# Opening a two-level matrix product with P1 and P2, and forming its operands one stage earlier

## The chip, the core and the metric

The program runs on one core of a Trainium2 chip. The metric is the device time of one execution in microseconds; the kernel before was timed at 2541.81 us (median of three runs, 2538.8 to 2543.2). The core has TensorE (PE in the rows, PEld for its weight loads), VectorE (DVE), ScalarE (ACT), GpSimd (POOL) and SyncE (SP, which here only issues transfers). Matmuls accumulate in PSUM, eight banks of 128 x 512 float32.

## The reference, cut to what matters

One layer of a streaming encoder on 512 rows and 2048 channels, in float32. Two branches share a normalised input h, and their gated sum is multiplied by w_out:

```
proj = h @ w_in                                  # also gives the gate logits
y_a = o_a @ w_br_a                               # branch A, gated DeltaNet
u = silu(layernorm(u)) * silu(z_b)
y_b = u @ w_br_b                                 # branch B
gate_a, gate_b = split(sigmoid(gate_logits + b_gate))
mixed = (gate_a * y_a + gate_b * y_b) @ w_out
x = x + rmsnorm(mixed, g_post)
x = x + rmsnorm(sigmoid(x @ w_ple_gate) * e, g_ple)
```

## The kernel before, in words

**Arithmetic.** Every float32 product is done as three fast matmuls: each operand is split into a high part (a cast on ACT) and a low part (a subtraction on DVE), and hi x hi, hi x lo and lo x hi are summed in PSUM. Weights arrive by SP's transfers into `raw` tiles (pool `rawp`, three buffers of 128 x 1024) and are split into `w` tiles (pool `ring`, four buffers).

**Stages and order.** Channel-major products run as jobs (`gemm_cm`, L160 on): 48 matmuls of 512 columns into one PSUM tile `g`, then an evacuation function. Pool `gps` has two such banks, so one job's evacuation lies beside the next job. Generators that were spawned are advanced by `tick`, once per matmul, and take a step every so many ticks. A scheduler orders each engine's instructions beforehand, by readiness and then by program order; an instruction whose output buffer isn't free is put behind others.

**Branch B** (L890 to L904) has 16 gate tiles (`gate_b_tile`, evacuated by a sigmoid on ACT, L700) and 16 tiles of y_b (`evac_yb`: L824 multiplies the PSUM tile by its gate, L826 adds it to `mixed`). Gate tiles run two ahead of the y_b tiles, so the normalised input `hT`, which fills all 32 buffers of `hpool`, is needed until almost the end. Gates lie in pool `slots` (21 buffers, 16 of them hold `mixed`). Pools `lop` (23 buffers, `LOP`) and `s2` (17 buffers) hold, in this stage, the 32 split tiles of u (`uh`, `ul`).

**The w_out product** is done by two levels of halving, for two column pairs `jp` one after the other: seven products P1, Q5, P6, P7, P3, P2, Q4 in place of eight. Left operands are sums of quarters of `mixed` (A11, S1 to S4, A12, A22), formed by `split_a`, `split_b` and `split_c` (L845 to L888), the first of them at the end of branch B, the others beside the first products. Right operands are blocks b11, b12, b22, b21 of w_out or running sums of them (`t`, pool `s3`): t1 = b11 + b12 by a DVE addition of two loaded tiles (L972), the later ones by an accumulating transfer that POOL issues (`acc`, L964). Each 128 x 1024 right operand is split into a piece (L1016 on ACT, L1017 on DVE) that feeds 12 matmuls (L1040 to L1042). `rw` is one more load buffer, in `s3`. Pool `s3` lies where `lop` and `s2` were, and is free only when the last y_b tile's matmuls have ended.

## Time and profile before

| | |
|---|---|
| median of three runs | 2541.81 us |
| the profiled execution, its own time | 2539.74 us |
| its span, first to last instruction | 2537.1 us |
| TensorE busy | 2495.0 us (98%) |
| VectorE busy | 1652.4 us (65%) |
| ScalarE busy | 1056.8 us (42%) |
| TensorE's mean granted clock | 0.997 |

The time is read off one profiled execution. A busy share is a mean over the whole span, and stages differ: windows of the span show which engine is short of what where. A matmul's record is longer than the distance to the next one, since matmuls overlap; the distance of their starts is what counts, and idle time in a row is therefore a little less than the time lost.

### The profile page before, as it was taken

To read this page: it belongs to the slowest core of one execution; us is meant where nothing else is said; L and a number is where in the kernel's file an instruction comes from. 1 tells how busy PE (TensorE), PEld (TensorE's weight loads), DVE (VectorE), ACT (ScalarE), POOL (GpSimd) and SP (SyncE) were. 2 spreads that over 40 slices of the span, in tenths; PEclk is the share of its full clock that TensorE was granted. 3 is DMA by queue.
4 is the path that set the end of the run, shared out by engine and by line. 5 is a ranking of instruction groups with operands and counts; after the bars stand their busy time and mean duration, and the time that the engine had idled before them with its cause. 6 is when DMAs were issued, how large, how long until landed. Compare 5 with 4: busy or idle time off the path is not lost.

```text
span 2537.1 us, 32634 instructions
## 1 busy us (share of the span) xinstructions
PE 2495.0 (98%) x12202; PEld 2035.7 (80%) x12202; DVE 1652.4 (65%) x3092; ACT 1056.8 (42%) x2083; POOL 140.6 (6%) x151
## 2 busy tenths in 40 slices
PE   8999999999999999999999999999999999999998
PEld 7878787777878777888888888887888888787887
DVE  6765767666676765977786868947433334777644
ACT  6655455455555455322222222225422222544532
POOL 0100000000000000000000000002000000000000
PEclk9999999999999999999999999999999999999999
DMA  6322222222222222333333332442322332677552
GB/s 257 122 87 71 84 72 83 79 75 88 71 84 71 84 67 75 104 105 102 105 97 107 104 107 98 135 135 92 100 99 93 100 99 92 184 214 224 191 174 75
DMA packets 85406, 279.45 MB, mean 110 GB/s; under 512 B 9472, under 2 KB 9728, under 8 KB 85248
## 3 DMA queue, kind: packets, MB, share of 16 engines
q1 hardware_dynamic: 81792, 266.89, 31.5%
q0 software_dynamic: 2304, 8.39, 1.8%
q10 hardware_dynamic: 1152, 2.10, 0.3%
q8 instruction: 95, 1.56, 0.3%
q14 instruction: 63, 0.52, 0.1%
HBM read 262.66 MB, written 14.68 MB: 109 GB/s over the span
## 4 chain that ended last, share of the span: by engine, by line
PE 85%; DVE 9%; ACT 2%; issue 2%; DMA 1%; POOL 0%; SPq 0%; DVEq 0%; POOLq 0%; ACTq 0%
PE g L182 23%; PE g L180 23%; PE g L178 23%; DVE prod L591 2%; PE f L1197 2%; PE f L1198 2%; PE f L1196 2%; DVE w L126 2%; PE psS L469 1%; PE f L1041 1%; PE f L1042 1%; PE f L1040 1%; DVE VT L592 1%; DVE cv L406 1%; PE psB L464 1%
## 5 line engine op out<-in xcount | busy, mean ns | idle before, releaser
L182 PE MATMUL g<-hh,w 128*128 128x512 f32 x2320 | 919.4, 396 | 13.1 <-DVE w L126 13.1
L180 PE MATMUL g<-hl,w 128*128 128x512 f32 x2320 | 915.2, 394 | 0.0
L178 PE MATMUL g<-hh,w 128*128 128x512 f32 x2320 | 914.6, 394 | 0.0
L126 DVE TENSOR_TENSOR w<-raw,w 128x512 fp32r<-128x512 f32 x780 | 549.2, 707 | 483.9 <-ACT w L125 482.8
L125 ACT CAST w<-raw 128x512 fp32r<-128x512 f32 x780 | 478.4, 619 | 893.3 <-PE g L182 789.3
L182 PEld LDWEIGHTS g<-hh,w 128*128 128x128 f32 x2320 | 436.6, 188 | 106.6 <-DVE w L126 21.2
L180 PEld LDWEIGHTS g<-hl,w 128*128 128x128 f32 x2320 | 436.6, 188 | 87.3 <-issue 1.6
L178 PEld LDWEIGHTS g<-hh,w 128*128 128x128 f32 x2320 | 436.8, 188 | 82.9 <-issue 0.2
L673 DVE SCALAR_TENSOR_TENSOR uc<-sg,vec,uc 128x483 f32<-128x483 f32 (+15 forms) x480 | 351.3, 734 | 14.2 <-ACT uc L670 4.3
L406 DVE SCALAR_TENSOR_TENSOR cv<-g,vec,cv 128x511 f32<-128x511 f32 x144 | 107.0, 743 | 32.9 <-ACT cv L404 32.3
L178 PE MATMUL g<-oh,w 128*128 128x512 f32 x256 | 99.6, 389 | 0.0
L180 PE MATMUL g<-ol,w 128*128 128x512 f32 x256 | 99.6, 389 | 0.0
L182 PE MATMUL g<-oh,w 128*128 128x512 f32 x256 | 99.6, 389 | 0.0
L178 PE MATMUL g<-uh,w 128*128 128x512 f32 x256 | 99.6, 389 | 0.0
L180 PE MATMUL g<-ul,w 128*128 128x512 f32 x256 | 99.6, 389 | 0.0
L182 PE MATMUL g<-uh,w 128*128 128x512 f32 x256 | 99.6, 389 | 0.0
L591 DVE TENSOR_TENSOR prod<-UT,VT 128x2 f32<-128x2 f32 (+30 forms) x248 | 87.6, 353 | 7.2
L1041 PE MATMUL f<-wsp,oph 128*128 128x512 f32 x192 | 76.7, 400 | 4.2 <-DVE wsp L1017 4.2
L1197 PE MATMUL f<-w,xh 128*128 128x512 f32 x192 | 75.6, 394 | 2.0 <-DVE w L126 2.0
L1040 PE MATMUL f<-wsp,oph 128*128 128x512 f32 x192 | 75.0, 398 | 1.8 <-ACT wsp L1016 1.8
L1196 PE MATMUL f<-w,xh 128*128 128x512 f32 x192 | 75.8, 396 | 0.0
L1042 PE MATMUL f<-wsp,opl 128*128 128x512 f32 x192 | 75.8, 395 | 0.0
(298 smaller groups left out, 2682.4 us busy)
## 6 DMA issues: line engine op xcount, KB each, us to landing
raw<-in_w_in SPq DMA_DIRECT2D x290, 512.0 KB, 3.3
raw<-in_w_ple_gate SPq DMA_DIRECT2D x40, 512.0 KB, 4.1
raw<-in_w_out SPq DMA_DIRECT2D x35, 512.0 KB, 4.8
raw<-in_w_br_a SPq DMA_DIRECT2D x32, 512.0 KB, 3.3
raw<-in_w_br_b SPq DMA_DIRECT2D x32, 512.0 KB, 3.2
t<-in_w_out POOLq DMA_DIRECT2D x16, 512.0 KB, 7.0
rw<-in_w_out SPq DMA_DIRECT2D x9, 512.0 KB, 4.7
x<-in_x SPq DMA_DIRECT2D x8, 512.0 KB, 9.1
```

The costliest lines, as they stand in the source:

```text
L125: nc.scalar.copy(hi, rq)
L126: nc.vector.tensor_tensor(lo, rq, hi.bitcast(F32), ALU.subtract)
L178: mm(ps, wh, rh, start=(k == 0), stop=False)
L180: mm(ps, wh, rl, start=False, stop=False)
L182: mm(ps, wl, rh, start=False, stop=(k == NK - 1))
L406: nc.vector.scalar_tensor_tensor(y[:, s:], ps[:, 0:T - s], vv(w0 + 3 - s), y[:, s:], ALU.mult, ALU.add)
L591: nc.vector.tensor_tensor(pv_, um, vm, ALU.mult)
L673: nc.vector.scalar_tensor_tensor(y[:, s:], u[:, 0:T - s], vv(w0 + TAPS - 1 - s), y[:, s:], ALU.mult, ALU.add)
L1041: mm(ps, lh, wl[:, c], start=False, stop=False)
L1042: mm(ps, ll, wh[:, c], start=False, stop=kk == 7)
L1196: mm(ps[tt], lh, wh, start=k == 0, stop=False)
L1197: mm(ps[tt], lh, wl, start=False, stop=False)
```

## The change

What it does, part by part. Branch B: gate tiles run eight ahead (`AHEAD`), and each further gate tile comes after a y_b tile and not before it; the first two gates lie in `slots`, the other 14 in `s2`. After the ninth y_b tile a generator `split_mixed`, one step every 12 matmuls, forms nearly all left operands of three of four row groups (`combine`); the fourth group and the splits of S3 follow beside the first products of w_out, two steps per piece. For the first column pair, w_out's products run as P1 with P2 (plain loads of b11 and b21), then Q5 alone, then P6, P7, P3, then Q4 alone; t1 is formed by a plain transfer of b12 into `t` and an accumulating transfer of b11, with no DVE addition. Entries hand over their transfers when they are started, up to two entries ahead, and their additions when they are used. The second column pair keeps its products and DVE additions; its reload of x (`load_x_again`) goes to `slots` and not `hpool`, and stands after P6 and P3. In layer norm, `rstd` moves from `s2` to `lop` and one more `ul` tile (ten, not nine) to `s2`.

```diff
@@ -694,9 +694,9 @@
-    def evac_gate(dst, i, col):
+    def evac_gate(dst, i, col, pool=None):
         def f(ps):
-            gt = slots.tile([P, T], F32, tag="s", name="gt")
+            gt = (pool or slots).tile([P, T], F32, tag="s2" if pool else "s", name="gt")
             nc.scalar.activation(gt, ps, AF.Sigmoid, bias=vv(V_BG + col))
@@ -788,7 +788,7 @@
-        rstd = s2.tile([P, T], F32, tag="s2", name="rstd")
+        rstd = low(0, "rstd", F32)
...
-            ul = low(LOP if i < 32 - LOP else 0, "ul")
+            ul = low(LOP if i < 33 - LOP else 0, "ul")
@@ -842,63 +842,69 @@
-    def split_a():
...
+    def halves(k2):
+        for n in range(2):
+            yield 2 * k2 + n, slice(n * 256, n * 256 + 256)
+
+    def combine(k2):
+        ah = hpool.tile([P, T], F32R, tag="h", name="ah")
+        al = hpool.tile([P, T], F32R, tag="h", name="al")
+        for kk, c in halves(k2):
+            while not (kk in added and kk + 8 in added):
+                yield
+            nc.scalar.copy(ah[:, c], mixed[kk][:, LO])
+            nc.vector.tensor_tensor(al[:, c], mixed[kk][:, LO], ah[:, c].bitcast(F32), ALU.subtract)
+            yield
+        AW["A11"][k2] = (ah, al)
+        for kk, c in halves(k2):
+            CC[kk] = sw_split(hpool, "h", mixed[kk + 8])
+            yield
+        s1 = slots.tile([P, T], F32, tag="s", name="sf")
+        for kk, c in halves(k2):
+            nc.vector.tensor_tensor(s1[:, c], mixed[kk][:, HI], mixed[kk + 8][:, HI], ALU.subtract)
+        AW["S1"][k2] = sw_split(hpool, "h", s1)
+        yield
+        s3_ = slots.tile([P, T], F32, tag="s", name="sf")
+        s4 = slots.tile([P, T], F32, tag="s", name="sf")
+        for kk, c in halves(k2):
+            nc.vector.tensor_tensor(s3_[:, c], mixed[kk][:, LO], mixed[kk][:, HI], ALU.subtract)
+            nc.vector.tensor_tensor(s1[:, c], s1[:, c], mixed[kk][:, LO], ALU.subtract)
+        yield
+        for kk, c in halves(k2):
+            nc.vector.tensor_tensor(s4[:, c], mixed[kk + 8][:, LO], s1[:, c], ALU.add)
+        AW["S2"][k2] = sw_split(slots, "s", s1)
+        yield
+        AW["S4"][k2] = sw_split(slots, "s", s4)
+        Sf[k2] = s3_
+        yield
+
+    def split_mixed():
+        for k2 in range(3):
+            yield from combine(k2)
+
+    def split_s3():
         for k2 in range(4):
...
+            AW["S3"][k2] = sw_split(s3, "s3", Sf.pop(k2))
             yield
 
     order = [k + 8 * n for k in range(8) for n in range(2)]
 
-    def gate_b_tile(i):
-        gemm_cm(w_in_tile(GATE_TILE0 + 16 + i), hT, evac_gate(gate_b, i, 16 + i))
-
-    gate_b_tile(order[0])
-    gate_b_tile(order[1])
+    AHEAD = 8
+
+    def gate_b_tile(i, pool):
+        gemm_cm(w_in_tile(GATE_TILE0 + 16 + i), hT, evac_gate(gate_b, i, 16 + i, pool))
+
+    gate_b_tile(order[0], None)
+    gate_b_tile(order[1], None)
     jobs.append(finish)
+    for n in range(2, AHEAD):
+        gate_b_tile(order[n], s2)
     for n, i in enumerate(order):
-        if n + 2 < NK:
-            gate_b_tile(order[n + 2])
-        elif n == NK - 2:
-            jobs.append(lambda: spawn(split_a(), 6, "mix"))
         gemm_cm(A["w_br_b"][i], uT, evac_yb(i))
+        if n + AHEAD < NK:
+            gate_b_tile(order[n + AHEAD], s2)
+        elif n + AHEAD == NK:
+            jobs.append(lambda: spawn(split_mixed(), 12, "mix"))
@@ -943,61 +949,78 @@
     entries = deque()
+    started = deque()
+    loads = [0]
+
     def load(jp, blk, q):
         loads[0] += 1
-        if early[0] or loads[0] % 4:
+        if loads[0] % 4:
             raw = rawp.tile([P, 1024], F32, tag="raw", name="raw", bufs=3)
         else:
             raw = s3.tile([P, 1024], F32, tag="rw", name="rw", bufs=1)
         nc.sync.dma_start(raw, WO[jp, blk, q])
         return raw
 
-    early = [True]
-    loads = [0]
-
     def acc(t, jp, blk, q):
         nc.gpsimd.dma_start(t, WO[jp, blk, q], accum_op=ALU.add)
 
-    def e_a(jp, q):
-        early[0] = jp == 0
+
+    def e_p1p2(jp, q):
+        two = [load(jp, B11, q), load(jp, B21, q)]
+        return lambda: two
+
+    def sum_t1(jp, q):
         b11 = load(jp, B11, q)
         b12 = load(jp, B12, q)
-        early[0] = False
+
+        def f():
+            t = tb[q] = s3.tile([P, 1024], F32, tag="t", name="t", bufs=4)
+            nc.vector.tensor_tensor(t, b11, b12, ALU.add)
+            return [b11, t]
+        return f
+
+    def e_q5(jp, q):
         t = tb[q] = s3.tile([P, 1024], F32, tag="t", name="t", bufs=4)
-        nc.vector.tensor_tensor(t, b11, b12, ALU.add)
-        return [b11, t]
+        nc.sync.dma_start(t, WO[jp, B12, q])
+        acc(t, jp, B11, q)
+        return lambda: [t]
 
     def e_63(jp, q):
         acc(tb[q], jp, B22, q)
-        return [tb[q], load(jp, B22, q)]
-
-    def sum_t3(jp, q, b22):
-        b12 = load(jp, B12, q)
+        b22 = load(jp, B22, q)
+        return lambda: [tb[q], b22]
+
+    def sum_t3(b12, b22):
         nc.vector.tensor_tensor(b12, b12, b22, ALU.add)
         return b12
 
     def e_b(jp, q):
         acc(tb[q], jp, B22, q)
         b22 = load(jp, B22, q)
-        return [tb[q], sum_t3(jp, q, b22), b22]
+        b12 = load(jp, B12, q)
+        return lambda: [tb[q], sum_t3(b12, b22), b22]
 
     def e_p7(jp, q):
-        return [sum_t3(jp, q, load(jp, B22, q))]
+        b22 = load(jp, B22, q)
+        b12 = load(jp, B12, q)
+        return lambda: [sum_t3(b12, b22)]
 
     def e_p2(jp, q):
         acc(tb[q], jp, B21, q)
-        return [load(jp, B21, q)]
+        b21 = load(jp, B21, q)
+        return lambda: [b21]
+
+    def e_q4(jp, q):
+        acc(tb[q], jp, B21, q)
+        return lambda: [tb[q]]
 
     def e_t(jp, q):
-        return [tb[q]]
-
-    def e_c(jp, q):
-        return e_p2(jp, q) + [tb[q]]
+        return lambda: [tb[q]]
 
     def split_piece():
         src = sources.popleft()
@@ -1005,7 +1028,7 @@
         count[0] += 1
         two = []
         for m in range(2):
-            if n < 8:
+            if n < 9:
                 two.append(ring.tile([P, 1024], F32R, tag="w", name="wsp") if n % 3 < 2 else
                            s3.tile([P, 1024], F32R, tag="wx", name="wsp", bufs=5))
             elif n % 2 == 0:
@@ -1019,9 +1042,11 @@
 
     def next_piece_sw():
         ahead = 3 if count[0] < 10 else 4
-        while len(pieces) < ahead and (sources or entries):
-            while len(sources) < 2 and entries:
-                sources.extend(entries.popleft()())
+        while len(pieces) < ahead and (sources or entries or started):
+            while len(sources) < 2 and (entries or started):
+                while entries and len(started) < 2:
+                    started.append(entries.popleft()())
+                sources.extend(started.popleft()())
             split_piece()
         return pieces.popleft()
 
@@ -1102,7 +1127,7 @@
-                xr[tt, j] = unit(HP_, "xr")
+                xr[tt, j] = unit(SLOT, "xr")
                 nc.sync.dma_start(xr[tt, j], rows(A["x"], tt, j))
@@ -1134,28 +1159,32 @@
-    for e, jp in ((e_a, 0), (e_b, 0), (e_c, 0), (e_a, 1), (e_63, 1), (e_p2, 1), (e_p7, 1), (e_t, 1)):
+    for e, jp in ((e_p1p2, 0), (e_q5, 0), (e_b, 0), (e_q4, 0), (sum_t1, 1), (e_63, 1), (e_p2, 1), (e_p7, 1), (e_t, 1)):
         stage(e, jp)
 
-    gen = split_b()
-    ps = run(("P1", "Q5"), stepper(gen))
+    def opening():
+        yield from combine(3)
+        yield from split_s3()
+
+    gen = opening()
+    ps = run(("P1", "P2"), stepper(gen, 2))
     drain(gen)
     s1 = [snap(S3_, x) for x in ps["P1"]]
-    s5 = [snap(S3_, x) for x in ps["Q5"]]
+    c11 = [add(unit(S3_, "c11"), ps["P2"][t], s1[t]) for t in range(2)]
     gp = [bcast_row(A["g_post"], j) for j in (0, 1)]
     fin = out_fin(0, gp)
-    gen = split_c()
-    ps = run(("P6", "P7", "P3"), stepper(gen))
-    drain(gen)
-    u2 = [add(unit(S3_, "u2"), ps["P6"][t], s1[t]) for t in range(2)]
+    for t in range(2):
+        fin(t, 0, c11[t])
+    ps = run(("Q5",))
+    s5 = [snap(S3_, x) for x in ps["Q5"]]
+    ps = run(("P6", "P7", "P3"))
+    u2 = [add(s1[t], ps["P6"][t], s1[t]) for t in range(2)]
     d = [minus(unit(S3_, "d"), s5[t], u2[t]) for t in range(2)]
     u3 = [add(u2[t], ps["P7"][t], u2[t]) for t in range(2)]
     for t in range(2):
         fin(t, 1, add(d[t], ps["P3"][t], d[t]))
         fin(2 + t, 1, minus(s5[t], s5[t], u3[t]))
-    ps = run(("P2", "Q4"))
-    for t in range(2):
-        fin(t, 0, add(s1[t], ps["P2"][t], s1[t]))
+    ps = run(("Q4",))
     for t in range(2):
         fin(2 + t, 0, add(u3[t], ps["Q4"][t], u3[t]))
 
@@ -1164,8 +1193,8 @@
     s5 = [snap(SLOT, x) for x in ps["Q5"]]
     gp = [bcast_row(A["g_post"], j) for j in (2, 3)]
     fin = out_fin(1, gp)
+    ps = run(("P6", "P3"))
     xr = load_x_again(LOW)
-    ps = run(("P6", "P3"))
     u2 = [add(unit(SLOT, "u2"), ps["P6"][t], s1[t]) for t in range(2)]
     for t in range(2):
         d = minus(unit(SLOT, "d"), s5[t], u2[t])
```

## Rows read from the trace of the kernel before

**Rows 1.** The page: span, TensorE's line (busy, share, instructions), VectorE's line.

```profile
span 2537.1 us, 32634 instructions
PE 2495.0 (98%) x12202; PEld 2035.7 (80%) x12202; DVE 1652.4 (65%) x3092; ACT 1056.8 (42%) x2083; POOL 140.6 (6%) x151
```

**Rows 2.** Windows, TensorE: stretch, us, busy (matmuls), granted clock, DMA share, GB/s.

```profile
2040.00:2175.00 135.00, 135.00 (x597) 1.00 0.28 94
2177.00:2212.00 35.00, 31.11 (x127) 1.00 0.89 235
2212.00:2310.00 98.00, 98.00 (x428) 1.00 0.80 227
2310.00:2327.00 17.00, 14.87 (x59) 0.90 0.69 217
2327.00:2355.00 28.00, 25.22 (x120) 0.94 0.54 180
```

**Rows 3.** Timeline of TensorE (start, duration) where tiles change: gate to y_b, y_b to w_out.

```profile
2099.64 0.39 PE L182 MATMUL g<-hh,w 128*128 128x512 f32 x1
2099.87 0.39 PE L178 MATMUL g<-uh,w 128*128 128x512 f32 x1
...
2175.80 0.39 PE L182 MATMUL g<-uh,w 128*128 128x512 f32 x1
2177.07 0.47 PE L1040 MATMUL f<-wsp,ah 128*128 128x512 f32 x1 [0.88 <-DVE gt L824]
```

**Rows 4.** Timeline of VectorE after a y_b tile's end; idle before, releaser in brackets.

```profile
2165.35 0.69 DVE L824 TENSOR_TENSOR gt<-g,gt 128x512 f32<-128x512 f32 x1 [1.33 <-PE g L182]
...
2166.06 0.69 DVE L126 TENSOR_TENSOR w<-raw,w 128x512 fp32r<-128x512 f32 x1
...
2166.67 0.69 DVE L826 TENSOR_TENSOR gt<-gt 128x512 f32<-128x512 f32 x1
```

**Rows 5.** Waits of TensorE, 2177 to 2212: who for whom, us, times, longest.

```profile
PE f L1041 <- DVE wsp L1017: 2.1, 4, 0.7
PE f L1040 <- ACT wsp L1016: 1.8, 3, 1.0
PE f L1040 <- DVE gt L824: 0.9, 1, 0.9
```

**Rows 6.** Windows, all engines: branch B's second half, then w_out's opening.

```profile
2040.00:2165.00 125.00, 125.00 (x553) 103.52 (x552) 47.47 (x80) 35.08 (x61) 0.00 (x0) 1.00 0.29 97
...
2177.00:2212.00 35.00, 31.11 (x127) 23.24 (x128) 32.67 (x49) 20.29 (x30) 4.54 (x5) 1.00 0.89 235
```

**Rows 7.** Groups by line, 1850 to 2250: count, busy us, mean ns, idle before.

```profile
L1017 DVE TENSOR_TENSOR wsp<-raw,wsp 128x1024 fp32r<-128x1024 f32 x13 | 15.9, 1221 | 3.3 <-PE g L182 2.6 <-ACT wsp L1016 0.6
...
L1016 ACT CAST wsp<-raw 128x1024 fp32r<-128x1024 f32 x13 | 13.5, 1047 | 16.0 <-PE g L182 7.4 <-PE f L1041 3.5 <-DMA raw<-in_w_out 3.1
...
L842 DVE TENSOR_TENSOR opl<-sf,oph 128x512 fp32r<-128x512 f32 x16 | 10.9, 686 | 0.2 <-ACT oph L840 0.2
...
L972 DVE TENSOR_TENSOR t<-raw 128x1024 f32<-128x1024 f32 x5 | 6.1, 1220 | 2.1 <-DMA raw<-in_w_out 2.1
...
L871 DVE TENSOR_TENSOR sf<-gt 128x256 f32<-128x256 f32 x8 | 3.1, 418 | 0.0
```

**Rows 8.** The page's transfer queues: packets, MB, share of 16 engines' span.

```profile
q1 hardware_dynamic: 81792, 266.89, 31.5%
q0 software_dynamic: 2304, 8.39, 1.8%
```

**Rows 9.** Timeline: SP's issue of the first rw load, and its use on VectorE.

```profile
2176.27 0.33 SPq L957 DMA_DIRECT2D rw<-in_w_out  x1
...
2208.26 1.22 DVE L981 TENSOR_TENSOR rw<-rw,raw 128x1024 f32<-128x1024 f32 x1
```

**Rows 10.** Timeline of TensorE at a stall in the second column pair, and an early one.

```profile
170.17 0.50 PE L182 MATMUL g<-hh,w 128*128 128x512 f32 x1 [1.25 <-DVE w L126]
...
2317.86 0.40 PE L1040 MATMUL f<-wsp,oph 128*128 128x512 f32 x1
2320.40 0.50 PE L1041 MATMUL f<-wsp,oph 128*128 128x512 f32 x1 [2.13 <-DVE wsp L1017]
```

**Rows 11.** Windows, TensorE, around stalls: us, busy (matmuls), granted clock, DMA share, GB/s.

```profile
166.00:172.00 6.00, 4.75 (x21) 1.00 0.14 42
...
2190.00:2196.00 6.00, 5.02 (x22) 1.00 0.84 245
...
2321.50:2325.50 4.00, 4.00 (x12) 0.57 0.84 279
```

More of the change, by code (lines that the diff above doesn't have):

```diff
@@ L843, in sw_split @@
         return hi, lo
-    def split_a():
-        for k2 in range(4):
-            ah = hpool.tile([P, T], F32R, tag="h", name="ah")
-            al = hpool.tile([P, T], F32R, tag="h", name="al")
-            s1 = slots.tile([P, T], F32, tag="s", name="sf")
-            for n in range(2):
-                kk = 2 * k2 + n
-                while not (kk in added and kk + 8 in added):
-                    yield
-                c = slice(n * 256, n * 256 + 256)
-                nc.vector.tensor_tensor(s1[:, c], mixed[kk][:, HI], mixed[kk + 8][:, HI], ALU.subtract)
-                nc.scalar.copy(ah[:, c], mixed[kk][:, LO])
-                nc.vector.tensor_tensor(al[:, c], mixed[kk][:, LO], ah[:, c].bitcast(F32), ALU.subtract)
-                yield
-            Sf[k2] = s1
-            AW["A11"][k2] = (ah, al)
-            AW["S1"][k2] = sw_split(hpool, "h", s1)
-            yield
@@ L864, in split_b @@
-    def split_b():
-        for k2 in range(4):
-            s1 = Sf.pop(k2)
-            s3_ = s3.tile([P, T], F32, tag="s3", name="sf")
-            for n in range(2):
-                kk = 2 * k2 + n
-                c = slice(n * 256, n * 256 + 256)
-                nc.vector.tensor_tensor(s3_[:, c], mixed[kk][:, LO], mixed[kk][:, HI], ALU.subtract)
-                nc.vector.tensor_tensor(s1[:, c], s1[:, c], mixed[kk][:, LO], ALU.subtract)
-            AW["S3"][k2] = sw_split(hpool, "h", s3_)
-            yield
-            AW["S2"][k2] = sw_split(hpool, "h", s1)
-            for n in range(2):
-                kk = 2 * k2 + n
-                c = slice(n * 256, n * 256 + 256)
-                nc.vector.tensor_tensor(s1[:, c], mixed[kk + 8][:, LO], s1[:, c], ALU.add)
-            AW["S4"][k2] = sw_split(slots, "s", s1)
-            yield
@@ L883, in split_c @@
-    def split_c():
-        for kk in range(8):
-            CC[kk] = sw_split(*((slots, "s") if kk < 4 else (s3, "s3")), mixed[kk + 8])
+    def halves(k2):
[32 more added lines that the diff above has]
+        yield
```

## The prediction

> **What bounds the kernel now.** I read the page's busy line first: TensorE is busy for 2495.0 of 2537.1 us [rows 1]. So there are some 40 us of gaps in all, and an edit pays only where it closes gaps, or costs where it opens new ones. The windows of TensorE show where they lie near the change [rows 2]: none in branch B's second half (597 matmuls in 135 us, one per 0.226 us), many in the opening of w_out, none from 2212 to 2310, two more spots after that. In the opening only 127 matmuls start in 35 us, where 35 / 0.226 = 155 would fit: 28 x 0.226 = 6.3 us are lost. (The idle time, 3.9 us, is less, because a matmul's record is longer than its share of the stream.) TensorE's waits there name a low part (L1017) four times and a high part (L1016) three times [rows 5], and VectorE is busy 32.67 of these 35 us [rows 6]: the opening is short of VectorE. What the change can win at this place is at most those 6.3 us. One more loss of 1.04 us lies just before it, where the last y_b tile hands over to w_out [rows 3]: starts at 2175.80 and 2177.07 are 1.27 apart, less 0.23. It waits for L824, the multiplication that frees the PSUM bank. The change doesn't touch it, but it gives me a price for what follows.
>
> **Branch B, operands.** From the tenth y_b tile on, `combine` steps every 12 matmuls: 7 tiles x 48 / 12 = 28 steps for 3 x 8 that are wanted, so three of four groups are done before w_out. One group costs VectorE ten half-width operations of 0.418 us and five splits of 0.686 us [rows 7], 7.6 us in 8 x 12 x 0.226 = 21.7 us (35%). VectorE stood at 47.47 of 125 us before [rows 6], 38%, which includes both evacuation operations and the weights; with 35% added it stays under 75%. I cost the moved operands at nothing: that slack hides them. Without it each group would cost its 7.6 us. `hpool` is free in time, since the last gate tile ends one y_b tile earlier. Moving `rstd` and one `ul` between pools costs no instruction.
>
> **Branch B, the gates' buffers.** Here I see a new wait. Pool `s2` has 17 buffers; ten `ul` tiles now stay in them to the end of branch B, so seven are left for gates. Gates 0 and 1 lie in `slots`. After y_b tile 0, gates 2 to 8 fill the seven. Gate 9 ends when y_b tile 1 has freed only a buffer of `slots`; its sigmoid must wait until y_b tile 2 has used up gate 2. Meanwhile gate 9 keeps one of the two PSUM banks and y_b tile 2 takes the other, so the next job has no bank until L824 of tile 2 has run. The same holds for gates 9 to 15: seven handovers, before gates 10 to 15 and before y_b tile 9, with no second bank. Usually a handover costs nothing (2099.64 to 2099.87, one ordinary step [rows 3]). Without a bank its nearest row is the handover to w_out, the same multiplication with TensorE waiting: 1.04 us [rows 3]. VectorE is idle when a y_b tile ends and starts L824 at once [rows 4], so I take 1.04 each: **7 x 1.04 = +7.3 us**. The bounds are 0 (should the buffers suffice after all) and 7 x (1.04 + 0.69) = +12.1, if a low part is ahead of L824 each time (0.69 us [rows 4]). On ScalarE the casts of the next weights lie behind the waiting sigmoid in program order; the scheduler puts them ahead, and three prepared half-pieces of 12 x 0.226 = 2.7 us each cover them. The waiting sigmoid itself ends about 2 us after L824 starts (L824, L126 and L826 in turn [rows 4], then the sigmoid), long before the next tile wants that bank.
>
> The Trainium skill (Perfetto Trace Analysis, section "Matmuls") asks that independent groups rotate through PSUM banks, so that one's evacuation lies beside the next one's matmuls. By that rule branch B loses its rotation here; by the kernel's second bank alone it would not, and the sum would be 7.3 us lower. Rows 3 show both cases in this trace, 0 and 1.04 us.
>
> **The opening, VectorE.** Four additions L972 (1.22 us each [rows 7]) go, and three quarters of the operand work is done already. What is left in P1 and P2 (8 pieces x 12 x 0.226 = 21.7 us): seven low parts of 1.22 = 8.5, the last group 7.6, four splits of S3 2.7, the last evacuation 1.4, together 20.2 us, and S3 may run later. So VectorE no longer sets the pace, and **-6.3 us** is open to be won.
>
> **The opening, transfers.** The plain transfers take 31.5% of 2537.1 us for 266.89 MB, or 1.57 us of all 16 engines per 512 KB; the accumulating ones 1.8% for 16 of them, 2.85 us each [rows 8]. The change adds four of these (t1). Transfers are issued as soon as their buffer is free: the first rw load went out at 2176.27, right when `s3` became free, and was used at 2208.26 [rows 9]. So I expect the four `t` loads there too, in SP's queue ahead of w_out's load 6 and behind load 4, with POOL's four accumulations soon after. In the 21.7 us of P1 and P2 the engines then have loads 4, 6, 7, 8, four `t` and four accumulations: 8 x 1.57 + 4 x 2.85 = 24.0 us of work. That is 2.3 us too much, and I take **+2.3 us** back, as late pieces of P2 and P1. The bounds are 0 (`t` loads behind the pieces') and 6.3 (as much as now). Q5 comes 21.7 us after the start and finds its sums ready. P6 needs the second accumulation on each `t`, which waits for Q5's split; in the 38 us of Q5 and P6, P7, P3 there is room for it.
>
> **The second column pair.** Its products and additions stay; its stalls (rows 2, last two lines) are at its end. One of them, 2317.86 to 2320.40, lost 2.31 us, and the half clock after it (12 matmuls in 4 us and not 17.7 [rows 11]) 1.3 more [rows 10, 11]. The reload of x now waits for `slots`; up to five of its tiles can be loaded earlier, beside P7's weights: at 0.79 us per 256 KB, half of 1.57, up to +3.9. That stall may also vanish: -3.6. No row favours a sign, so I take 0 and keep both for the range.
>
> **Sum:** 7.3 - 6.3 + 2.3 = **+3.3 us**. On the profiled execution's 2539.74 us that is 2543.0; the median of the runs is 2541.81, 2.1 above it, so I predict 2545.1 us, 0.13% slower. About 0.2% (5.1 us) is what a measurement of this kernel can tell from no change: below 2536.7 counts as faster, above 2546.9 as slower.
>
> **Rivals.**
> (a) The handovers cost nothing, because a buffer is free that I count as taken. Then -6.3 + 2.3 = -4.0, 2537.8 us; with punctual transfers -6.3, 2535.5. For it: no gap at any handover in branch B now [rows 2, 3]. Against: 10 + 7 of 17 buffers leave none over. Chance 0.15.
> (b) Slower: the opening becomes bound by transfers and loses as much as before, +7.3, 2549.1 us. It decides when load 6 lands less than 2.3 us (a high part 1.05, a low part 1.22 [rows 7]) before its product is due. For it: the transfer engines are at 0.89 already [rows 2]. Against: half the loads of P1 and P2 are issued before branch B ends. Chance 0.25.
> (c) TensorE's clock falls at each handover. A fall costs 1.3 us [rows 11], so 7 x 1.3 = 9.1 more: 2554.2 us. In this trace the waits of 1.25 us at 170.17 [rows 10] and the small ones at 2190 stayed at 1.00, which is 2.4 GHz, and the fall to half, 1.2 GHz, came after the 2.31 us loss [rows 10, 11]. The Trainium skill (TensorE: Matmul & The Clock Gate, "A second HAM failure mode: psum-queue depth-cycling") describes such a fall from short idle times between groups that cycle through PSUM; the rows here speak against it at this length. Chance 0.05.
> (d) The change doesn't bring the operands in time, because `combine` lags behind its steps; each missing group then puts 7.6 us of VectorE back into the opening. 28 steps for 24 speak against it; it would end as (b), and is counted there.
>
> **How the numbers follow.** My forecast has 0.50, (a) 0.15, (b) 0.25, (c) 0.05; 0.05 is left for the second pair moving by more than 3 us either way. Faster by over 0.2% is part of (a), the half with punctual transfers, and a little of the rest: 0.10. Slower is (b), (c) and the tail of the forecast: 0.35. The rest, 0.55, is within 0.2%. The range reaches from 2538 (most of (a)) to 2552 ((b) with the second pair 3 us worse); (c), and (a) with punctual transfers, are left out.
>
> **What would show it.** In TensorE's timeline of branch B: seven gaps of about 1.27 us between starts, 21.7 us apart, each released by L824; if they aren't there, (a) holds. In the opening: 35 us windows with some 145 matmuls and waits for L1016 after transfers, not for L1017. VectorE clearly under 90% there, and no L972 before the second column pair. POOL's first accumulations within 6 us of the last y_b tile. The prediction is wrong if the handovers cost more than the multiplication, or if the w_out loads stand ahead of the `t` loads and the opening is clean.

## The result

The changed kernel took 2552.48 us (median of six runs, 2549.78 to 2554.96) where the kernel before took 2541.38 (six runs beside them): a ratio of 1.0046, with a 95% interval of 1.0033 to 1.0059. It is 11.1 us slower, where 3.3 were forecast, and lies just above the range. The profiled execution took 2550.99 us, 11.25 more than the one before.

First the page of the changed kernel (span; TensorE and VectorE lines), then TensorE's windows (us, busy with matmuls, granted clock, DMA share, GB/s). The first window holds branch B where the handovers are; the second begins with w_out; the last two answer to the last two of rows 2.

```profile
span 2549.2 us, 32652 instructions
PE 2498.7 (98%) x12202; PEld 2037.6 (80%) x12202; DVE 1649.8 (65%) x3088; ACT 1058.8 (42%) x2083; POOL 144.4 (6%) x155
```

```profile
1960.00:2110.00 150.00, 143.87 (x629) 1.00 0.27 92
...
2186.00:2221.00 35.00, 30.69 (x120) 0.90 0.95 266
2221.00:2319.00 98.00, 97.04 (x422) 1.00 0.83 227
2319.00:2336.00 17.00, 14.67 (x57) 0.89 0.81 280
2336.00:2364.00 28.00, 25.89 (x122) 0.94 0.35 123
```

TensorE is busy for 3.7 us more over the span [rows 1], and the gaps grew besides. Branch B, without a gap before [rows 2], now has them; the opening runs 120 matmuls in 35 us, fewer than the 127 before, part of them at a lower clock.

By the starts in TensorE's timeline, the last matmul of w_out begins at 2358.13 and not 2345.54, 12.59 us later. w_out begins 8.89 later (2185.96 for 2177.07), of which 7.9 are new handovers and 1.0 was lost long before them (it is there by the hundredth matmul, 32 us after the start); the first column pair takes 86.12 us for 83.08 (+3.04), the second 86.05 for 85.39 (+0.66).

**Branch B.** TensorE's waits from 1960 to 2110 (who for whom, us, times, longest), and one of the seven handovers in its timeline (start, duration):

```profile
PE g L178 <- DVE gt L824: 6.1, 7, 0.9
```

```profile
2084.53 0.39 PE L182 MATMUL g<-uh,w 128*128 128x512 f32 x1
2085.80 0.47 PE L178 MATMUL g<-hh,w 128*128 128x512 f32 x1 [0.88 <-DVE gt L824]
```

Seven waits for L824 as forecast, each 1.27 between starts, so 1.04 lost, 22.9 us apart; the next matmul is 0.08 late too, together some 7.9 us.

**The opening.** In the changed kernel a piece's cast is L1039, its low part L1040 and its matmuls L1065 to L1067 (in the experiments these lines lie a little further down). TensorE's waits from 2186 to 2221 (the last row is the handover to w_out, as in rows 5), its timeline at the stall, ScalarE's timeline across it, and TensorE's windows by clock:

```profile
PE f L1065 <- ACT wsp L1039: 3.4, 1, 3.4
PE f L1066 <- DVE wsp L1040: 0.9, 1, 0.9
PE f L1065 <- DVE gt L824: 0.9, 1, 0.9
```

```profile
2205.02 0.39 PE L1067 MATMUL f<-wsp,al 128*128 128x512 f32 x1
2208.77 0.50 PE L1065 MATMUL f<-wsp,oph 128*128 128x512 f32 x1 [3.36 <-ACT wsp L1039]
2210.22 0.79 PE L1066 MATMUL f<-wsp,oph 128*128 128x512 f32 x1 [0.95 <-DVE wsp L1040]
```

```profile
2206.73 1.04 ACT L1039 CAST wsp<-t 128x1024 fp32r<-128x1024 f32 x1 [7.46 <-DMA t<-in_w_out]
2207.68 1.04 ACT L1039 CAST wsp<-rw 128x1024 fp32r<-128x1024 f32 x1
2210.64 1.04 ACT L1039 CAST wsp<-t 128x1024 fp32r<-128x1024 f32 x1 [1.92 <-DMA t<-in_w_out]
```

```profile
2204.00:2209.40 5.40, 1.91 (x8) 1.00 1.06 274
2209.40:2216.20 6.80, 5.98 (x14) 0.50 1.05 261
```

TensorE waited at 2205 for the last piece of P2, from `rw`. By its transfer's record that load had landed at 2198.97; but its cast stands behind the cast of Q5's first `t` in ScalarE's queue, and that one waited 7.46 us for its accumulation. Then come the piece's own low part and 6.8 us at half clock (0.50, 1.2 GHz).

Transfers in the opening, first of the changed kernel (2186 to 2221): the queue of the accumulations (packets, MB, share of 16 engines), then issues (transfer, queue, number, KB, median us from issue to landing). The second fence has the issues of the kernel before (2177 to 2212).

```profile
q0 software_dynamic: 806, 2.98, 42.8%
...
t<-in_w_out POOLq DMA_DIRECT2D x7, 512.0 KB, 10.7
raw<-in_w_out SPq DMA_DIRECT2D x5, 512.0 KB, 10.0
```

```profile
raw<-in_w_out SPq DMA_DIRECT2D x10, 512.0 KB, 4.8
t<-in_w_out POOLq DMA_DIRECT2D x5, 512.0 KB, 5.8
```

SP's issues in the opening of the changed kernel, then two of POOL's:

```profile
2189.97 0.33 SPq L966 DMA_DIRECT2D raw<-in_w_out  x1
2190.34 0.90 SPq L989 DMA_DIRECT2D t<-in_w_out  x2
2194.66 0.33 SPq L966 DMA_DIRECT2D rw<-in_w_out  x1
2195.32 0.80 SPq L989 DMA_DIRECT2D t<-in_w_out  x2
2196.18 3.89 SPq L966 DMA_DIRECT2D raw<-in_w_out  x3
```

```profile
2196.25 1.97 POOL L970 DMA_DIRECT2D t<-in_w_out  x2 [443.57 <-DMA t<-in_w_out]
...
2206.96 0.88 POOL L970 DMA_DIRECT2D t<-in_w_out  x1 [4.33 <-DMA t<-in_w_out]
```

The second of these POOL rows is the fourth accumulation. Its own plain load had landed at 2202.74, but it went out only at 2206.96, 0.26 us after the first accumulation had landed, and the next two followed the landings of the second and third in the same way. So no more than three accumulations are in flight, and the fourth starts 4.2 us later than its load allowed. No run tests what this costs by itself; e14, further down, has a clean opening in spite of it.

An accumulation still costs 2.6 us of all engines (0.428 x 35 us for 2.98 MB, per 0.524 MB), about the 2.85 of rows 8. What doubled, near enough, is the time to land.

### The profile page after: what moved, and what is told of

It reads as the page before. It is cut to its first block, busy times and chain, and to the rows that moved or that the text cites. A ratio compares the mean times of both kernels' runs of the same rounds, so it can differ in the third digit from the quotient of the medians.

```text
span 2549.2 us, 32652 instructions
## 1 busy us (share of the span) xinstructions
PE 2498.7 (98%) x12202; PEld 2037.6 (80%) x12202; DVE 1649.8 (65%) x3088; ACT 1058.8 (42%) x2083; POOL 144.4 (6%) x155
## 4 chain that ended last, share of the span: by engine, by line
PE 86%; DVE 8%; issue 2%; ACT 2%; DMA 1%; POOL 0%; SPq 0%; DVEq 0%; POOLq 0%; ACTq 0%
PE g L182 23%; PE g L180 23%; PE g L178 23%; DVE prod L591 2%; PE f L1227 2%; PE f L1225 2%; PE f L1226 2%; DVE w L126 2%; PE f L1066 1%; PE psS L469 1%; PE f L1067 1%; PE f L1065 1%; DVE VT L592 1%; DVE cv L406 1%; PE psB L464 1%
## 5 line engine op out<-in xcount | busy, mean ns | idle before, releaser
L1065 PE MATMUL f<-wsp,oph 128*128 128x512 f32 x192 | 77.3, 404 | 4.5 <-ACT wsp L1039 4.5
L1067 PE MATMUL f<-wsp,opl 128*128 128x512 f32 x192 | 77.4, 404 | 0.0
L1226 PE MATMUL f<-w,xh 128*128 128x512 f32 x192 | 75.0, 390 | 2.1 <-DVE w L126 2.1
L1227 PE MATMUL f<-w,xl 128*128 128x512 f32 x192 | 74.9, 390 | 0.0
```

The lines of the kernel that those rows point to most:

```text
L1067: mm(ps, ll, wh[:, c], start=False, stop=kk == 7)
L1226: mm(ps[tt], lh, wl, start=False, stop=False)
L1227: mm(ps[tt], ll, wh, start=False, stop=k == NK - 1)
```

## The experiments

Two losses were to be explained: the handovers, and an opening that lost 9.2 us where 2.3 were forecast. "Opening" in the table is the time from the start of w_out's first matmul to that of its 145th (after P1, P2 and Q5; in the kernel before, e5 and e6 after P1, Q5 and a third of P6, P7 and P3), less 144 x 0.2267 us; "pair" is the same over the 336 matmuls of the first column pair; both are from TensorE's timeline in the profiled run. Ratios are to the kernel before in the same runs.

| kernel | median us | ratio, 95% interval | handovers | opening | pair |
|---|---|---|---|---|---|
| before | 2541.4 | | 0 | 6.3 | 6.9 |
| changed | 2552.5 | 1.0046 [1.0033, 1.0059] | 7 | 9.2 | 9.9 |
| e1 gate 9 in `slots` | 2544.0 | 1.0008 [0.9999, 1.0017] | 0 | 8.3 | 9.1 |
| e2 order of one cast | 2552.0 | 1.0039 [1.0027, 1.0052] | 7 | 11.4 | 12.2 |
| e3 t1 on VectorE | 2551.2 | 1.0035 [1.0023, 1.0047] | 7 | 10.4 | 12.9 |
| e4 no accumulation | 2543.5 | 1.0008 [0.9999, 1.0017] | 7 | 0.3 | 1.1 |
| e5 P1 and Q5 first | 2551.5 | 1.0035 [1.0023, 1.0048] | 7 | 11.1 | 11.6 |
| e6 = e5 + e1 | 2542.9 | 1.0007 [0.9998, 1.0016] | 0 | 10.1 | 10.6 |
| e7 `t` loads first | 2559.9 | 1.0071 [1.0057, 1.0085] | 7 | 13.0 | 16.4 |
| e8 half accumulations | 2554.2 | 1.0049 [1.0036, 1.0061] | 7 | 12.2 | 13.6 |
| e9 = e2 + early g_post | 2552.4 | 1.0045 [1.0033, 1.0058] | 7 | 11.3 | 12.0 |
| e10 = e9 + e1 | 2545.3 | 1.0017 [1.0008, 1.0026] | 0 | 11.9 | 12.6 |
| e11 P6 loads held | 2553.7 | 1.0045 [1.0032, 1.0059] | 7 | 11.6 | 12.7 |
| e12 = e10 + e11 | 2546.9 | 1.0027 [1.0018, 1.0036] | 0 | 12.8 | 15.7 |
| e13 all in order | 2547.6 | 1.0025 [1.0016, 1.0034] | 7 | 4.8 | 6.1 |
| e14 = e13 + e11 | 2547.6 | 1.0024 [1.0014, 1.0034] | 7 | 0.1 | 4.4 |
| e15 = e14 + e1 | 2538.4 | 0.9989 [0.9981, 0.9998] | 0 | 0.1 | 3.9 |
| e16 = e13 + e1 | 2538.8 | 0.9993 [0.9985, 1.0002] | 0 | 5.0 | 6.5 |
| e17 = e15, shorter hold | 2536.7 | 0.9985 [0.9977, 0.9994] | 0 | 0.3 | 2.9 |

### The handovers: e1

```diff
-            gate_b_tile(order[n + AHEAD], s2)
+            gate_b_tile(order[n + AHEAD], None if n + AHEAD == 9 else s2)
```

> The changed kernel (2552.5 us), with one edit: gate tile 9 gets its buffer from slots, not s2, so that s2's seven free buffers never run out. Bank theory (each of gates 9 to 15 keeps a PSUM bank until a later y_b tile frees a buffer, 1.04 us between the tiles and a little more in the next matmul): all seven gaps in branch B go, 7.3 to 7.9 us less, 2544.6 to 2545.2. Rival (the gaps come from VectorE being late with the multiplication, now that it forms operands in this stage): the gaps stay, 2552.5.

Measured 2544.04 us, 8.4 below the changed kernel, a little more than the bank theory's 7.3 to 7.9. The same window of branch B as above:

```profile
1960.00:2110.00 150.00, 150.00 (x663) 1.00 0.29 96
```

One gate in another pool, and all seven waits are gone (663 matmuls for 629). The chain of the prediction is shown: gate 9 has no buffer, keeps a PSUM bank, and the debt is handed on to y_b tile 9. In the later pairs of runs that differ in this edit alone it gives 8.5 (e6 to e5), 7.1 (e10 to e9), 9.2 (e15 to e14) and 8.7 (e16 to e13): it adds up with whatever the opening does.

### Is it the accumulations? e2, e3, e4

e2 puts the cast and the low part of the eighth piece (the `rw` above) ahead of those of the ninth, the first `t`; e3 loads b11 and b12 plainly and adds on VectorE; e4 leaves out the accumulation of b11 into `t`, a part of the sum.

```diff
 e3:
-        nc.sync.dma_start(t, WO[jp, B12, q])
-        acc(t, jp, B11, q)
...
+        nc.vector.tensor_tensor(t, b11, b12, ALU.add)
 e4:
-        acc(t, jp, B11, q)
```

> The changed kernel (2552.5 us), with one edit: the cast and subtraction of the first t1 piece are ordered on ScalarE and VectorE behind those of the last P2 piece; in the changed kernel ScalarE's order is the other way, and the last P2 piece, landed at 2199.0, is cast only at 2207.7, after t1's cast, which waits until 2206.7 for an accumulating transfer. Order theory (that order costs the whole opening's loss, 9.2 us over P1, P2 and Q5, the clock's fall included): some 8 us less, 2544.5. Landing theory (the four accumulations, 10 to 13 us each and the last landed at 2219.0, set when Q5 can end: 2219.0 + 2.3 for the split + 2.7 for 12 matmuls = 2224.0 where it was 2227.8): 3.7 us less, 2548.8.

> The changed kernel (2552.5 us), with one edit: t1 of the first column pair is formed as before, from two plain loads by an addition on VectorE (1.22 us each), in place of a plain and an accumulating transfer. Transfer theory (the accumulations' time in the transfer engines made the opening's loss): 6 to 9 us less, 2543.5 to 2546.5, no fall of the clock. VectorE theory (the change won what it could by taking the additions off VectorE, and they bring back the stalls of before): 9.2 us of loss become 6.3, 2549.6.

> The changed kernel (2552.5 us), with t1's accumulating transfer left out: t1 is b12 alone, so that Q5 is formed with a wrong right operand; all else is computed as before. It prices these four transfers. Transfer theory: the opening is clean but for 1 us, 8 to 9 us less, 2543.5 to 2544.5. If the plain transfers alone were too much for the stage, half of the loss stays: 2548.

e4: 2543.54 us, 8.9 less, and its opening is clean:

```profile
2187.00:2222.00 35.00, 35.00 (x154) 1.00 0.93 263
```

The engines are as full as in the changed kernel (0.93 for 0.95), yet no matmul is late. So full transfer engines are not enough for a loss; something must wait for a late one. e2 (2552.01) and e3 (2551.23) gave next to nothing, against both theories. In e2 the loss of P1 and P2 fell (the first 96 matmuls lost 1.9 us, not 7.4), but Q5 lost 9.5 where it had lost 1.8. In e3 VectorE waited 3.4, 2.7 and 3.3 us at additions for late loads; what of its loss lies in that order, and what in two loads for each piece of Q5, isn't separated.

### How much, when, and beside what: e5 to e8

e5 opens w_out with P1 and Q5 as before (t1 again by VectorE's addition, and P2 beside Q4), e6 adds e1's edit to it. e7 issues the four `t` loads and accumulations when `s3` opens. e8 accumulates half the columns, and so leaves out half of that sum.

```diff
 e5:
-    ps = run(("P1", "P2"), stepper(gen, 2))
+    ps = run(("P1", "Q5"), stepper(gen, 2))
...
 e7:
+    first = [entries[4 + q]() for q in range(4)]
...
 e8:
-        acc(t, jp, B11, q)
+        nc.gpsimd.dma_start(t[:, 0:T], WO[jp, B11, q][:, 0:T], accum_op=ALU.add)
```

> The changed kernel, but w_out begins with P1 and Q5 again and t1 of the first column pair is added on VectorE from the two plain loads (as it still is in the second pair); P2 goes back beside Q4. The operands stay in branch B and the gates stay as changed, so the seven handovers of 1.04 us stay too. The changed kernel took 2552.5 us and lost 9.9 us in the first column pair. Transfer theory (the opening of the changed kernel is short of transfer engines, which stand at 1.0 from 2190 to 2228 us): the opening now needs five plain loads, 7.9 us of all engines, in 21.7 us, with no accumulation of its own, and the loss falls to 1 to 2 us: 2544 to 2546 us. VectorE theory (the opening is short of VectorE whatever the transfers do): 20.2 us of work as in the prediction, four additions of 1.22 and one more low part of 1.22 make 26.3 us in 21.7, a loss of 4 to 5 us: 2547 to 2549 us.

> The run with P1 and Q5 first, and gate 9 in slots as well, so that no gate waits for a buffer of s2. If the two causes are separate and add up, this is 8.4 us under the run with P1 and Q5 first (the gain of gate 9 by itself): 2535.5 to 2537.5 us by the transfer theory, 2538.5 to 2541 by the VectorE theory. If they are not separate (the earlier start of w_out finds its transfers less ready), the gain of gate 9 shrinks here to under 6 us: 2538 us or more also with a clean opening.

> The changed kernel, with the four plain transfers into t and the four accumulations of the first column pair issued right when s3 opens, ahead of load 4 on SP's queue (in the changed kernel they went out 5 to 10 us later, behind loads that waited for a raw buffer, while the transfer engines were at 0.37 in the first 5 us). Idle-start theory (the engines have too little time because they begin late): the accumulations land before Q5 is due, 3 to 6 us of the loss of 9.9 go, 2546.5 to 2549.5 us. Rival (the engines have too much work over P1 and P2 in any order): the pieces of P1 and P2 are late in place of Q5's, the loss stays within 1.5 us, 2551 to 2554 us.

> The changed kernel, with only the first 512 of 1024 columns of b11 accumulated into each t of the first column pair (256 KB in place of 512 KB, four times; the other half of the sum is left out). Leaving all four out gave 2543.5 us, the changed kernel 2552.5. If the price of the accumulations is the transfer engines' time (2.7 us of all engines for each 512 KB), half of it goes, 5.4 us of engine time, and the time lies midway or lower, since a shorter stall also spares the fall of the clock: 2544.5 to 2549 us. If it is a fixed cost of each accumulation (its issue on POOL, its place behind the plain transfer), the time hardly moves: 2551 to 2553 us.

None came out as a theory of amounts wants it: 2551.47, 2542.93, 2559.88 and 2554.20 us. VectorE's timeline in e5 (start, duration, idle before and releaser in brackets), and TensorE's at the same place:

```profile
2196.57 0.68 DVE L842 TENSOR_TENSOR opl<-sf,oph 128x512 fp32r<-128x512 f32 x1
2204.86 1.23 DVE L983 TENSOR_TENSOR t<-raw,rw 128x1024 f32<-128x1024 f32 x1 [7.60 <-DMA rw<-in_w_out]
2206.01 0.75 DVE L871 TENSOR_TENSOR sf<-sf,gt 128x256 f32<-128x256 f32 x2
2206.68 1.22 DVE L1045 TENSOR_TENSOR wsp<-t,wsp 128x1024 fp32r<-128x1024 f32 x1
...
2207.95 0.80 PE L1071 MATMUL f<-wsp,oph 128*128 128x512 f32 x1 [7.42 <-DVE wsp L1045]
```

The low part that TensorE needs was ready to run when its cast ended, at 2196.6. It stands behind an addition that waits 7.60 us for a late load. In e7 it is ScalarE, in e8 VectorE behind the broadcast of g_post:

```profile
2202.18 1.04 ACT L1039 CAST wsp<-t 128x1024 fp32r<-128x1024 f32 x1 [7.09 <-DMA t<-in_w_out]
2205.40 1.04 ACT L1039 CAST wsp<-t 128x1024 fp32r<-128x1024 f32 x1 [2.18 <-DMA t<-in_w_out]
2206.35 1.04 ACT L1039 CAST wsp<-rw 128x1024 fp32r<-128x1024 f32 x1
```

```profile
2224.07 1.29 DVE L1111 TENSOR_TENSOR c<-c,grow 128x512 f32<-128x512 f32 x2 [4.10 <-DMA grow<-in_g_post]
2225.28 1.22 DVE L1040 TENSOR_TENSOR wsp<-t,wsp 128x1024 fp32r<-128x1024 f32 x1
```

In e7 the `rw` load had landed at 2197.5, 8.8 us before its cast. In e8 half the accumulating did shorten the first stall (from 3.5 to 1.1 us lost); then this wait cost 5.4 us, and the clock fell after each. That gave a new theory: late transfers hurt through the order in which ScalarE and VectorE were told beforehand to take their work.

### Single remedies, and their sum: e9 to e12

e9 is e2 with the two broadcasts of g_post loaded when w_out opens; e10 adds e1's edit. e11 holds the first four loads for P6 and P7 until Q5's second and third cast; e12 is all of it.

```diff
 e9:
+    gp = [bcast_row(A["g_post"], j) for j in (0, 1)]
     gen = opening()
...
 e11:
+        if 9 <= loads[0] <= 12:
+            nc.scalar.copy(raw[:, 0:1], pieces[-1][0].bitcast(F32)[:, 0:1])
         nc.sync.dma_start(raw, WO[jp, blk, q])
```

> The changed kernel with the casts of w_out's pieces in the order of their products (as in the run on the order, 2552.0 us) and, in addition, the two broadcasts of g_post loaded when w_out opens, not after P2. In the run on the order alone, VectorE waited 2.18 us for a broadcast (grow) with the low part of a piece behind that multiplication, and TensorE lost 4.3 us there and then ran at half clock. Queue theory (an instruction that waits for a late transfer keeps ready work on its engine from running, in turn on ScalarE and on VectorE): with both such places gone Q5 is paced by the landings of its accumulations alone, 3.5 us apart, and the first column pair loses 5 to 7 us, not 12: 2546 to 2548.5 us. Rival (the accumulations set the end of Q5 and P6 whatever stands in the queues): the wait only moves, 2551 to 2553 us.

> The run with the casts in order and the broadcasts early, with gate 9 in slots as well. If the seven handovers in branch B and the opening are separate costs, this is 8.4 us under that run: 2537.5 to 2540.5 us by the queue theory, 2542.5 to 2545 by the rival. If an earlier start of w_out finds its transfers less ready, the gain of gate 9 is under 6 us.

> The changed kernel, but the first four plain loads for P6 and P7 (issued from 2196.2 us on in the changed kernel, 25 us before their products, beside the accumulations of Q5) wait until the second and third of Q5's pieces are cast: ScalarE writes one column of each buffer before its load, which overwrites it. Nothing is left out. Contention theory (transfers that are not yet needed share the engines with those that are): the first three accumulations land in 7 to 8 us and not in 10.5 to 13.5, the loss of the opening falls by 3 to 5 us: 2547.5 to 2549.5 us. Rival (three or four accumulations in flight are slow among themselves): within 1.5 us of the changed kernel, 2551 to 2554 us.

> All four together: gate 9 in slots, casts in order, broadcasts early, the loads for P6 and P7 held. If the costs are separate and the contention theory holds, 8.4 us of the handovers and 8 to 10 us of the opening go from 2552.5: 2534 to 2537 us, below the kernel before (2541.4). If the accumulations are slow among themselves, the hold gives nothing and this ends like the run without it, 2537.5 to 2540.5 us; if neither the order nor the broadcasts help, 2542 to 2545 us.

None came out by the theory that it was made for: 2552.40, 2545.33, 2553.66 and 2546.88 us. e9 and e11 lie in the spans of their rivals, e10 is 0.3 us above its rival's, and e12 is above every case that it named. ScalarE in e9, then VectorE in e11:

```profile
2209.94 1.05 ACT L1044 CAST wsp<-t 128x1024 fp32r<-128x1024 f32 x1 [3.46 <-DMA t<-in_w_out]
2210.89 0.58 ACT L1093 COPY snap<-f 128x512 f32<-128x512 f32 x1
2217.61 1.04 ACT L1044 CAST wsp<-t 128x1024 fp32r<-128x1024 f32 x1 [6.13 <-DMA t<-in_w_out]
2218.56 0.58 ACT L1093 COPY snap<-f 128x512 f32<-128x512 f32 x1
2219.04 1.05 ACT L1044 CAST wsp<-t 128x1024 fp32r<-128x1024 f32 x1
```

```profile
2211.61 0.68 DVE L1093 TENSOR_TENSOR c<-f,snap 128x512 f32<-128x512 f32 x1
2220.47 1.22 DVE L1001 TENSOR_TENSOR raw<-raw 128x1024 f32<-128x1024 f32 x1 [8.17 <-DMA raw<-in_w_out]
2221.61 0.68 DVE L1093 TENSOR_TENSOR c<-f,snap 128x512 f32<-128x512 f32 x1
2222.21 2.35 DVE L1042 TENSOR_TENSOR wsp<-t,wsp 128x1024 fp32r<-128x1024 f32 x2
```

In e9's ScalarE queue the cast of the fourth `t` stands ahead of the third's: the third landed at 2213.8, and both ran after the fourth had landed at 2217.5. In e11 the hold brought the accumulations sooner (they landed at 2204.3, 2206.8, 2209.3 and 2211.8, not 2206.7 to 2219.0, though the first three in 9.1 to 11.0 us and not the 7 to 8 expected), so its rival's number came without its rival's cause; P7's sum now waited 8.17 us on VectorE ahead of two low parts of accumulated tiles. Each remedy removed its own wait, and the next instruction that stood ahead of ready work took it over. The Trainium skill (PSUM — Partial Sum Buffer, "Engine vs sequencer instructions") says that the queues of ScalarE and VectorE are strictly first in, first out; these rows agree.

### The order on both engines: e13 to e17

e13 chains every cast and low part of the first column pair, from the fifth piece on, in the order of the products, places P7's sum directly ahead of its own cast, and does the last step of P2 after P6, P7 and P3. e14 adds e11's hold, e15 also e1's edit; e16 is e13 with e1's edit; e17 is e15 with the hold let go one cast earlier.

```diff
+        with ExitStack() as es:
+            if 4 <= n < 28:
+                es.enter_context(tc.issue_after(last[0]))
+                es.enter_context(tc.issue_after(last[1]))
+            if callable(src):
+                src = src()
+            c = nc.scalar.copy(hi, src)
+            s = nc.vector.tensor_tensor(lo, src, hi.bitcast(F32), ALU.subtract)
+        last[:] = [c.ins, s.ins]
...
-        return lambda: [tb[q], sum_t3(b12, b22), b22]
+        return lambda: [tb[q], lambda: sum_t3(b12, b22), b22]
...
```

> The changed kernel with every cast and low part of the first column pair's pieces from the fifth on in the order of the products, on ScalarE and on VectorE, the sums for P7 directly ahead of their own cast, and the last step of P2 (the multiplication by g_post) after P6, P7 and P3. In the two runs with a part of this (the order of one cast; the broadcasts early) the wait only moved, since the next cast or sum that stood ahead of ready work took it over (in the second the cast of the fourth accumulated tile stood ahead of the third's, 6.1 us of waiting on ScalarE). Queue theory: with no such place left Q5 is paced by the landings alone; with those of the changed kernel (the last at 2219.0, 33 us after the start) its last piece is ready at 2221.2 and Q5 ends at 2223.9, where 2218.6 would be without loss: 5.3 us are lost, not 9.2, and the first column pair loses 5.5 to 6.5: 2548 to 2549.5 us. Rival (the accumulations land late by as much as any order gains): 2551 to 2553 us.

> The same, with the first four loads for P6 and P7 held as in the run on the hold. There the four accumulations landed at 2204.3, 2206.8, 2209.3 and 2211.8 (10.5 to 13.5 us each became 7.3 to 11.0), but VectorE waited 8.2 us for the sum of P7 with a low part of Q5 behind it. Contention and queue together: Q5 loses under 1 us, P7's first sum is then late by some 3 us (its load landed at 2220.4 and 3.5 us of sum, cast and low part follow, where 2220.6 was due), the first column pair loses 3.5 to 5 us: 2546 to 2548 us. Rival (transfers only trade places): no better than without the hold.

> The same as the last, with gate 9 in slots as well, so that no handover in branch B waits. Separate costs: 8.4 us below it, 2537.5 to 2539.5 us, a little under the kernel before (2541). If an earlier start of w_out only adds to its waits, 2541 to 2545 us.

> The run with all in order, with gate 9 in slots as well and no load held. All in order alone took 2547.6 us, and so did all in order with the hold; with the hold and gate 9 it was 2538.4. If the two causes (seven handovers in branch B; ready work behind late transfers in the opening) are separate, this is 8.4 us under 2547.6: 2538.5 to 2540 us. If the hold is needed once w_out starts earlier, it is 2541 us or more.

> The run with all in order, the hold and gate 9, with the loads for P6 and P7 let go one accumulated piece earlier (after the first and the second of Q5's casts, not the second and the third). In that run the first column pair still lost 3.9 us, since P7's first sum came 2 to 3 us late (its load issued at 2201.2 landed at 2212.8). Let go 2.5 us earlier it would land 1 to 2.5 us earlier, while Q5's pieces, which had some 1.5 us to spare, come later by as much: 2536.5 to 2538.5 us. If the transfers only trade places, 2538 to 2540 us.

e13 took 2547.56 us, 4.9 less than the changed kernel, a little under the span that the queue theory gave and outside the rival's. The opening's windows in e13, then e14:

```profile
2186.00:2221.00 35.00, 32.16 (x135) 1.00 0.95 267
```

```profile
2185.00:2220.00 35.00, 34.85 (x152) 1.00 0.97 254
```

With the same transfers, as many engines busy and landings as late as in the changed kernel (the last at 2218.1), e13 loses 4.8 us in the opening and not 9.2, in four stalls of 0.6 to 1.4 us, one per piece of Q5, and the clock stays at 1.00. So of the 9.2 some 4.4 came from the order on the two engines and the clock that fell after it; 4.8 are the late landings themselves (5.0 in e16). How the 4.4 divide among e13's three edits and the clock isn't separated. e14 brings these to 0.1, but its P7 then loses some 3 us more behind the held loads, as expected; the median is the same, 2547.59 us, so the hold alone isn't shown to be worth anything. With gate 9 the two give 2538.44 (e15) and 2538.81 (e16), and e17 2536.67, each within its expected span. e15 and e17 are faster than the kernel before, by 0.11% and 0.15%, with intervals clear of 1; e17 is the best here, 15.8 us under the changed kernel. It lies 2.1 us under e16, which was timed beside it; resampling the medians of their eleven and twelve times gives 0.8 to 4.4, and the first pair's loss agrees (2.9 us for 6.5). So the shorter hold seems to be worth a little, while the longer one (e15 beside e16, e14 beside e13) isn't told apart from none.

## Why the prediction was wrong

**Branch B, operands at nothing: right.** VectorE has the slack (busy 65.3 of 135 us from 2049 on, under the 75% forecast): TensorE waits there for L824 alone, and in e1 for nothing.

**The handovers, +7.3: right**, in number, place and cause, and 0.6 too small: seven at 1.04, and 0.08 in the matmul after each that the sum left out, some 7.9. Rival (a) is out. So is rival (c): the granted clock stayed at 1.00 through all seven.

**The opening, VectorE, -6.3: right as far as it went.** The kernel before lost 6.28 us there, and the new opening is no longer short of VectorE (22.4 of 35 us busy, not 32.7 [rows 6]). e4 shows that nearly all of it could be had: 0.3 us lost. But it is won only if nothing else is late.

**The opening, transfers, +2.3: this step failed.** The opening lost 9.2 us, 6.9 more than forecast, and that is nearly the whole error of 7.95 in the profiled executions (11.25 for 3.3): the handovers' 0.6, the second pair's 0.7, 0.1 in the rest of the first and the 1.0 lost long before the handovers make 2.4 more, and 1.3 of it are gone again behind w_out. Three things were wrong in it. It counted work on the transfer engines in the 21.7 us of P1 and P2 as if it could start at once and as if nothing else were under way: the `t` loads went out at 2190.3 to 2195.7 and not when `s3` opened, behind loads on SP's queue that waited for a `raw` or `rw` buffer, and from 2196.2 on three loads for P6 and P7 shared the engines. The four accumulations took 10.5 to 13.5 us to land. The Trainium skill (DMA: Bandwidth & Descriptors, "Issuing engines are not separate DMA queues") says that transfers issued by different engines interleave on the same 16; e11 agrees, where the third accumulation took 9.1 us with those loads held, for 12.4. That the `t` loads went out late isn't shown to have cost anything by itself: e7 issued them at once and lost 13.0 us, with the order on ScalarE as it was. Then it asked only when a transfer lands, and not what stands behind the instruction that waits for it: e13 puts 4.4 us on that, the clock included. And its upper bound, "as much as now", had no reason. After a stall of 3.5 us the clock fell for 6.8 us; 14 matmuls from 2210.22 on took 6.07 us and not 3.17, so 2.9 more, which the forecast of the first pair didn't price. (The 38 us that this step gives Q5, P6, P7 and P3 are 43.5, 192 matmuls at 0.2267; no term hangs on it.)

**The second column pair at 0:** +0.7 in the profiled runs, within its bounds. One trace tells little here: with the same products in it, the second pair took 84.6 to 89.1 us in the traces of the experiments.

**Rival (b) was the case that came**, in sign and place. Its price, 2549.1 us, was too low by 3.4, since it took the loss of the kernel before as its size. Its test (when load 6 lands) was the wrong one: load 6 landed at 2190.2, some 9 us before its product was due, and the `rw` load 8.7 us before its cast ran. Nor was it transfers alone: by e13 about half of the loss was the order on the engines and the clock. The forecast's chance for slower, 0.35, was too small beside it.

**The signs named beforehand:** seven gaps, yes; VectorE under 90% and no t1 additions, yes; waits for a cast after transfers and not for low parts, in the main (3.4 us for a cast, but behind another piece's transfer, and 0.9 for a low part); some 145 matmuls in 35 us, no (120); POOL's first accumulation within 6 us of the last y_b tile, no (2196.25, more than 10 us).

## What to carry to other kernels

A transfer that lands late can cost more than its lateness: look on each in-order engine at which instruction waits for it and what ready work stands behind, since a remedy for one such wait only hands it to the next until the order of all of them follows the consumer. When a pool's buffers decide who may leave a PSUM bank, count them against all holders, as one gate in another pool was worth 8.4 us. Bound a step from above by its mechanism (landing, queue, clock), not by what the place costs today.

## What the runs showed of the hardware

Accumulating transfers of 512 KB took 5.4 to 7.4 us from issue to landing in the opening of the kernel before, and 10.5 to 13.5 us for the first four of the changed one, with up to three in flight and not two; three plain loads beside them took 10 to 14 us. This was at 2.6 us of engine time for each accumulation, 2.85 in rows 8. TensorE's clock held at 1.00 through seven gaps of 1.04 us in branch B and through e13's four stalls of 0.6 to 1.4 us within 13 us; in the changed kernel it fell at 2209.4, after the loss of 3.5 us and during the one of 1.2 behind it, and stood at 0.50 for 6.8 us. The size of a loss alone doesn't tell: 1.96 and 1.22 us in a row left it at 1.00 in e11, while 1.09 and 1.22 in a row were followed by 3.4 us at 0.50 in e8.
